# In the FFNs of a two-layer decoder trunk, block products are issued in pairs: wide halves together, narrow halves together, evacuations after

## The chip, the cores and the metric

The kernel runs on one core of one Trainium2 chip. The metric is the device time of one execution in microseconds (us), the median of several. PE is TensorE (matmuls), DVE is VectorE, ACT is ScalarE, POOL is GpSimd, SP is SyncE, which here issues DMAs. PSUM is the memory that PE writes its sums to, in banks of 512 columns of float32.

## The reference, cut to what matters

512 tokens of 1024 channels go through two layers. Each has a mixer and then a gated FFN of hidden width 2816:

```
def gated_conv_ffn(x, w_gate, w_up, conv_w, conv_b, w_down):
    g = jnp.einsum('bsd,df->bsf', x, w_gate)
    g = causal_dwconv3(g, conv_w) + conv_b
    up = jnp.einsum('bsd,df->bsf', x, w_up)
    return jnp.einsum('bsf,fd->bsd', jax.nn.silu(g) * up, w_down)
```

All of it is float32. In layer 0 the input is normalised by a factor of each token that the kernel multiplies in after the matmuls (`self.r`); in layer 1 the same, with one of the factors put into the last add.

## The kernel before, in words

**Precision.** A float32 factor is split in a high part and a low part, each of type float32r. A product of two such factors is made of three matmuls: high x high, high x low, low x high. The low part is either made by DVE as source minus high part (L153, L732, about 1.2 us for 128x1024), or by ACT's negated copy and a DMA that POOL issues, which adds the source (L142 to L144).

**Units of the FFN.** The 22 blocks of 128 hidden channels are taken two at a time: a unit `f` is blocks f and f + 1, for the gate ("g") and for the up-projection ("u"). Unit 0 is multiplied directly. Units 2 to 20 are multiplied by a scheme of seven block products in place of eight (2x2 blocks: halves of the 1024 input channels, and the two hidden blocks, against halves of the 512 tokens). The products are numbered 1 to 7. The sums of weight blocks which they need (s12, s34) are made by DVE (L752 to L775), split by ACT and DVE or by ACT and DMA, and sums of the input are made once a layer.

**A product** (`multiply`, L558 to L583) has four steps over the input channels, and adds into a PSUM bank: products 1, 6, 7 and 4 into bank "a", 5 and 3 into "e", 2 into "b", for g and u each their own. From unit 4 on for g and unit 6 for u (and three products of u in unit 4) the product is *wide*: four matmuls of 512 columns, in which the high weights meet high and low input at once (L571), then four of 256 columns, low weights with high input, into the first half of the bank (L574). Before that all twelve are 256 wide (L581).

**Evacuation** (`after`, L804 and L816). Since later products go on adding into the same bank, what it holds after each is read out: ACT copies the first half (products 1, 6, 5 and 4) and DVE adds the second half; for 2, 7 and 3 DVE adds both halves onto an earlier result. `rows` is the padded buffer of the gate, `kept` that of the up-projection. The next product into that bank has to wait for these reads.

**Order.** The products of a unit are written down as g1, u1, g2, g5, g6, u5, u6, g7, u2, u7, g3, u3, g4, u4, each with its evacuation straight behind it (L819 to L831). A scheduler then lays out the instructions of all engines by its own estimate of when each is ready; only instructions marked so keep program order. Each engine runs its list in order. After each unit from the second on comes a half of a down-projection of four earlier blocks (`half_down`: 48 matmuls of 512 columns, 12 into each of four banks), whose weights come in two chunks, each with a high split on ACT and a low split on DVE (L152, L153). There are seven banks in a pool for all of these.

**Buffers of the split weights.** High and low parts have six buffers each (`whi`, `wlo`), used in turn: a split waits until the matmuls that read the buffer's former contents are done.

Of the kernel before, what the change touches and what calls it, by code (L numbers as in the profile page):

```python
# [31 lines left out]
def tile_trunk(ctx: ExitStack, tc: tile.TileContext, x, norm_mix, norm_ffn, final_norm,  # L32
# [3 lines left out]
    nc = tc.nc  # L36
# [9 lines left out]
    def mm_bank(name):  # L46
        return ps_mm.tile([P, 512], F32, tag="mm", name=name)
# [240 lines left out]
    def padded_tile():  # L288
        turn[0] += 1
        return padded[turn[0] % NPADDED]  # L290
# [258 lines left out]
    NP = NK // 2  # L549
# [6 lines left out]
    last_matmul = [None]  # L556

    def multiply(banks, name, product, left, right, both=None):  # L558

        at = BANK[product]
        first = at not in banks
        if first:
            banks[at] = mm_bank(f"{name}{at}")
        ps = banks[at][:, :HALF]
        if both is not None:
            for kp in range(NP):  # L570
                nc.tensor.matmul(banks[at], left(kp)[0], both(kp), start=first and kp == 0,  # L571
                                 stop=kp == NP - 1, skip_group_check=True)
            for kp in range(NP):
                last_matmul[0] = nc.tensor.matmul(ps, left(kp)[1], right(kp)[0], start=False,  # L574
                                                  stop=kp == NP - 1, skip_group_check=True)
            return banks[at]
        for kp in range(NP):
            (a_hi, a_lo), (b_hi, b_lo) = left(kp), right(kp)
            for l, r, end in ((a_hi, b_hi, False), (a_hi, b_lo, False),
                              (a_lo, b_hi, kp == NP - 1)):  # L580
                nc.tensor.matmul(ps, l, r, start=first, stop=end, skip_group_check=True)  # L581
                first = False
        return ps  # L583

    def ffn_weights(layer, f, order):
        cs = slice(f * P, (f + 2) * P)
# [5 lines left out]
    class Ffn:  # L592
# [192 lines left out]
        def products(self, f, stat):  # L785

            layer, ap, n = self.layer, self.ap, f"{self.layer}_{f}"
            banks = {"g": {}, "u": {}}
            kept = ap.tile([P, 3, HALF], F32, tag="kept", bufs=1, name=f"kept{n}")
            pads = [padded_tile() for _ in range(2)]  # L790
            lo, hi = slice(2, 2 + HALF), slice(2 + HALF, 2 + S)
            dst = {("g", 1): pads[0][:, lo], ("g", 6): pads[0][:, hi], ("g", 7): pads[1][:, hi],
                   ("g", 4): pads[1][:, lo]}
            dst.update({("u", product): kept[:, i, :] for i, product in enumerate((1, 6, 7))})
            onto = {2: 1, 7: 7, 3: 6}
            s = {}

            def in_both(key, product):
                return f >= FIRST_WIDE[key] or f == FIRST_WIDE["g"] and product in (2, 5, 3)

            def add(d, bank, halves):
                ins = None
                for half in halves:
                    ins = nc.vector.tensor_tensor(d, bank[:, half * HALF : (half + 1) * HALF], d,  # L804
                                                  ALU.add)
                return ins

            def after(key, product, bank):
                halves = range(1 + in_both(key, product))
                if product in onto:  # L810
                    ins = add(dst[key, onto[product]], bank, halves)
                    if product == 7:
                        self.added[key] = ins
                elif (key, product) != ("u", 4):
                    d = dst[key, 7 if product == 5 else product]
                    nc.scalar.copy(d, bank[:, :HALF])  # L816
                    add(d, bank, halves[1:])

            for key, product in (("g", 1), ("u", 1), ("g", 2), ("g", 5), ("g", 6), ("u", 5),  # L819
                                 ("u", 6), ("g", 7), ("u", 2), ("u", 7), ("g", 3), ("u", 3),  # L820
                                 ("g", 4), ("u", 4)):
                bank = self.multiply(banks[key], f"{key}{n}", product, stat[key, product],
                                     in_both(key, product))
                after(key, product, bank)
                if (key, product) in (("g", 4), ("g", 3)):
                    j = product == 4
                    row = pads[j][:, 2:]
                    nc.vector.tensor_tensor(row, row, self.r, ALU.mult)  # L828
                    s[j] = self.silu(self.conv(pads[j], f + j), f + j)
                    if j and layer == 0:  # L830
                        nc.vector.tensor_tensor(s[1], s[1], self.r, ALU.mult)  # L831
            if layer == 0:
                nc.vector.tensor_tensor(kept[:, :2, :], kept[:, :2, :],
                                        self.r.rearrange("p (a b) -> p a b", a=2), ALU.mult)
            s0 = s[0].rearrange("p (a b) -> p a b", a=2)
            nc.vector.tensor_tensor(s0, kept[:, :2, :], s0, ALU.mult)
            nc.vector.tensor_tensor(s[1][:, HALF:], kept[:, 2, :], s[1][:, HALF:], ALU.mult)
            last = bank[:, :HALF]
            if in_both("u", 4):
                last = kept[:, 0, :]  # L840
                nc.scalar.copy(last, bank[:, :HALF])
                add(last, bank, (1,))
            nc.vector.tensor_tensor(s[1][:, :HALF], last, s[1][:, :HALF], ALU.mult)
            return [(f + 1, s[1]), (f, s[0])]
# [53 lines left out]
    def mixer1(norm):  # L898
        w = w_in_odd[0]
        with tc.tile_pool(name="m1", bufs=1) as mp:  # L900
# [27 lines left out]
            banks = v_group(0, {(4, 0): lambda: norm.rstd_cols(inorder)})  # L928
# [33 lines left out]
            def tokens(product, i):  # L962

                def at(kp):
                    if product in SUM:
                        cs = slice(i * P, (i + 1) * P)
                        return tuple(x[:, kp % 2, SUM[product], cs] for x in sums[kp // 2])
                    k = kp if product == 1 else kp + NP
                    cs = slice((i + 2 * (product == 4)) * P, (i + 2 * (product == 4) + 1) * P)
                    return hg[k][0][:, cs], hg[k][1][:, cs]  # L970
                return at

            class InProducts:
# [31 lines left out]
                def run(self, out_, done, behind_first):  # L1005
                    banks = ({}, {})
                    e = {}
                    for i, product in ((0, 1), (1, 1), (0, 2), (1, 2), (0, 6), (1, 6), (0, 5),
                                       (0, 7), (1, 5), (1, 7), (0, 4), (0, 3), (1, 4), (1, 3)):
                        if (i, product) == (0, 2):  # L1010
                            behind_first()
                        hi, lo = self.stat[product]
                        ps = multiply(banks[i], f"{self.name}_{i}", product, tokens(product, i),
                                      lambda kp: (hi[:, kp, :], lo[:, kp, :]))
                        c = {1: (0, 0), 2: (0, 0), 6: (0, 1), 3: (0, 1), 7: (1, 1), 5: (1, 1),
                             4: (1, 0)}[product]
                        dst = out_(i + 2 * c[0])[:, c[1] * HALF : (c[1] + 1) * HALF]
                        if product in (1, 6):
                            nc.scalar.copy(dst, ps)
                        elif product == 5:  # L1020
                            e[i] = ps
                        elif product == 7:
                            nc.scalar.copy(dst, ps)
                            nc.vector.tensor_tensor(dst, e[i], dst, ALU.add)
                            gelu(dst, dst, i + 2)
                        elif product == 4:
                            gelu(dst, ps, i + 2)
                            done(i + 2)
                        else:
                            nc.vector.tensor_tensor(dst, ps, dst, ALU.add)  # L1030
                        if product == 3:
                            row = out_(i)
                            gelu(row, row, i)
                            done(i)

            def gelu(dst, src, t):
                nc.scalar.activation(dst, src, AF.Gelu, scale=norm.cols[:, t : t + 1])
# [26 lines left out]
            u, gt, mix = {}, {}, {}  # L1064
# [334 lines left out]
    n = mixer0()  # L1399
    n = ffn0(n)  # L1400
    n = mixer1(n)
# [31 lines left out]
```

## Time and profile before

| | |
|---|---|
| median of 3 runs | 975.62 us (975.47 to 975.7) |
| span of the profiled execution, first to last instruction | 973.0 us |
| what lies around the span, against the median | 2.6 us |
| granted TensorE clock, mean | 0.998 |
| layer 0's FFN, units 2 to 20 | about 168 to 460 us |
| layer 1's FFN, units 2 to 20 | about 651 to 945 us |

The profile is of one execution; its own time is the span, and the runs are 2.6 us longer. In a line of the timeline stand the start in us from the span's start, the length in us, engine, line, operation, what is written and read, shape and count of the merged instructions, and in brackets the idle time before and what ended it. The length of a matmul is modelled and overlaps the next one; starts are what can be relied on. Buffer and layer numbers are left out of names: `g_12a` is bank "a" of g in unit 12, `whi_s12g` the high part of g's sums s12. A line of windows has the stretch, then busy time and count of PE, PEld (weight loads), DVE, ACT and POOL, then clock and DMA.

### The profile page before, as it was taken

To read this page: it belongs to the slowest core of one execution; us is meant where nothing else is said; L and a number is where in the kernel's file an instruction comes from. 1 tells how busy PE (TensorE), PEld (TensorE's weight loads), DVE (VectorE), ACT (ScalarE), POOL (GpSimd) and SP (SyncE) were. 2 spreads that over 40 slices of the span, in tenths; PEclk is the share of its full clock that TensorE was granted. 3 is DMA by queue.
4 is the path that set the end of the run, shared out by engine and by line. 5 is a ranking of instruction groups with operands and counts; after the bars stand their busy time and mean duration, and the time that the engine had idled before them with its cause. 6 is when DMAs were issued, how large, how long until landed. Compare 5 with 4: busy or idle time off the path is not lost.

```text
span 973.0 us, 14003 instructions
## 1 busy us (share of the span) xinstructions
PE 963.6 (99%) x5120; PEld 828.8 (85%) x5120; DVE 817.0 (84%) x1393; ACT 598.7 (62%) x905; POOL 149.9 (15%) x173
## 2 busy tenths in 40 slices
PE   9999999999999999999999999999999999999996
PEld 7888888988888888888889988889888888888885
DVE  5887458999899898998986865589998989889897
ACT  5523347765676665765487734587765667656775
POOL 2142023110111010110310001221111011100123
PEclk9999999999999999999999999999999999999999
DMA  7442225776777677774324623167767777668775
GB/s 251 146 139 86 87 88 108 178 178 165 195 178 181 146 178 185 174 174 140 119 58 110 221 67 99 55 132 187 186 145 194 196 173 172 156 165 201 194 153 140
DMA packets 94417, 148.36 MB, mean 152 GB/s; under 512 B 5156, under 2 KB 60428, under 8 KB 94348
## 3 DMA queue, kind: packets, MB, share of 16 engines
q1 hardware_dynamic: 78316, 98.69, 32.2%
q0 software_dynamic: 14256, 46.93, 26.7%
q10 hardware_dynamic: 1776, 1.84, 0.6%
q8 instruction: 40, 0.66, 0.3%
q14 instruction: 29, 0.24, 0.1%
HBM read 98.42 MB, written 2.10 MB: 103 GB/s over the span
## 4 chain that ended last, share of the span: by engine, by line
PE 99%; DVE 1%; issue 0%; ACT 0%; POOLq 0%; DVEq 0%; POOL 0%
PE dn L158 3%; PE d L158 3%; PE dn L159 3%; PE dn L157 3%; PE d L159 3%; PE d L157 3%; PE gu L157 2%; PE gu L159 2%; PE oo L159 1%; PE oo L157 1%; PE gu L158 1%; PE oe L157 1%; PE oe L159 1%; PE oo L158 1%; PE oe L158 1%; PE u_2a L581 1%
## 5 line engine op out<-in xcount | busy, mean ns | idle before, releaser
L617 DVE SCALAR_TENSOR_TENSOR c<-rows,prm,c 128x512 f32<-128x512 f32 x88 | 65.6, 748 | 1.5 <-ACT c L615 1.4
L144 POOL DMA_DIRECT2D wlo_g<-raw_g x20 | 17.2, 860 | 321.3 <-DVE kept L804 187.4
L158 PE MATMUL dn<-wlo_dn,a_hi 128*128 128x512 f32 x144 | 56.3, 391 | 0.0
L158 PE MATMUL d<-a_lo,whi_d 128*128 128x512 f32 x144 | 56.3, 391 | 0.0
L159 PE MATMUL dn<-whi_dn,a_lo 128*128 128x512 f32 x144 | 56.2, 391 | 0.0
L159 PE MATMUL d<-a_hi,wlo_d 128*128 128x512 f32 x144 | 56.2, 390 | 0.0
L157 PE MATMUL d<-a_hi,whi_d 128*128 128x512 f32 x144 | 56.2, 390 | 0.0
L157 PE MATMUL dn<-whi_dn,a_hi 128*128 128x512 f32 x144 | 56.2, 390 | 0.0
L731 ACT ACTIVATE whi_a<-raw_g 128x512 fp32r<-128x512 f32 x20 | 12.6, 631 | 61.0 <-PE g_10e L571 8.7
L213 POOL TENSOR_TENSOR ssq_f<-ssq_f,sq_f 128x512 f32<-128x512 f32 x14 | 19.8, 1411 | 134.4 <-ACT sq_f L212 99.5
L202 ACT ACTIVATE hg<-h,prm 128x512 fp32r<-128x512 f32 x24 | 17.3, 722 | 34.9 <-DVE h L315 34.9
L142 ACT ACTIVATE wlo_g<-raw_g 128x1024 fp32r<-128x1024 f32 x20 | 21.2, 1062 | 27.5 <-PE g_2e L581 8.8
L615 ACT ACTIVATE c<-rows,prm 128x512 f32<-128x512 f32 x44 | 31.3, 715 | 6.6 <-DVE rows L828 6.6
L1187 DVE SCALAR_TENSOR_TENSOR y<-dn,small,y 128x512 f32<-128x512 f32 x40 | 28.0, 749 | 8.6 <-PE dn L159 8.6
L625 ACT ACTIVATE s<-c,prm 128x512 f32<-128x512 f32 x44 | 31.4, 715 | 6.2 <-DVE c L617 6.1
L203 DVE SCALAR_TENSOR_TENSOR hg<-h,prm,hg 128x512 fp32r<-128x512 f32 x24 | 23.6, 986 | 11.1 <-ACT hg L202 11.1
L266 ACT ACTIVATE a_hi<-s 128x512 fp32r<-128x512 f32 x40 | 24.9, 627 | 11.4 <-PE d L159 7.7
L159 PEld LDWEIGHTS dn<-whi_dn,a_lo 128*128 128x128 f32 x144 | 27.1, 188 | 5.7
L159 PEld LDWEIGHTS d<-a_hi,wlo_d 128*128 128x128 f32 x144 | 27.1, 188 | 5.6
L153 DVE TENSOR_TENSOR wlo_dn<-raw_dn,whi_dn 128x1024 fp32r<-128x1024 f32 x18 | 22.0, 1224 | 11.7 <-ACT whi_dn L152 11.7
L157 PEld LDWEIGHTS dn<-whi_dn,a_hi 128*128 128x128 f32 x144 | 27.1, 188 | 5.3
L157 PEld LDWEIGHTS d<-a_hi,whi_d 128*128 128x128 f32 x144 | 27.1, 188 | 5.3
(1132 smaller groups left out, 3319.9 us busy)
## 6 DMA issues: line engine op xcount, KB each, us to landing
raw_g<-in_w_ffn_gate_dram SPq DMA_DIRECT2D x40, 512.0 KB, 3.8
raw_u<-in_w_ffn_up_dram SPq DMA_DIRECT2D x40, 512.0 KB, 4.0
raw_dn<-in_w_ffn_down_dram SPq DMA_DIRECT2D x22, 512.0 KB, 6.3
wlo_u<-raw_u POOLq DMA_DIRECT2D x21, 512.0 KB, 6.1
wlo_g<-raw_g POOLq DMA_DIRECT2D x20, 512.0 KB, 4.6
raw_d<-in_w_ffn_down_dram SPq DMA_DIRECT2D x18, 512.0 KB, 4.2
wlo_s12g<-s12g POOLq DMA_DIRECT2D x18, 512.0 KB, 6.3
wlo_s34g<-s34g POOLq DMA_DIRECT2D x18, 512.0 KB, 5.5
```

The source lines that it names most:

```text
L142: first = nc.scalar.activation(lo, raw, AF.Copy, scale=-1.0)
L153: behind(nc.vector.tensor_tensor(lo, raw, hi.bitcast(F32), ALU.subtract), after[0])
L157: nc.tensor.matmul(ps, lhs[0], rhs[0], start=start, stop=False)
L158: nc.tensor.matmul(ps, lhs[0], rhs[1], start=False, stop=False)
L159: nc.tensor.matmul(ps, lhs[1], rhs[0], start=False, stop=stop)
L203: nc.vector.scalar_tensor_tensor(hg[k][1], h[k], g, hg[k][0].bitcast(F32), op0=ALU.mult, op1=ALU.subtract)
L213: nc.gpsimd.tensor_tensor(self.ssq, self.ssq, sq, ALU.add)
L266: nc.scalar.activation(hi, src, AF.Copy, scale=scale)
L615: nc.scalar.activation(c, t[:, 0:S], AF.Copy, scale=prm("cf", ft))
L617: self.last_conv = nc.vector.scalar_tensor_tensor(c, t[:, i : S + i], prm("cf", i * NF + ft), c, op0=ALU.mult, op1=ALU.add)
L625: self.last_silu = nc.scalar.activation(s, c, AF.Silu, bias=self.prm("bf", ft))
L1187: return nc.vector.scalar_tensor_tensor(dst, ps, ffn.cols[:, t : t + 1], dst, op0=ALU.mult, op1=ALU.add)
```

## The change

`multiply` no longer issues the narrow matmuls of a wide product itself. It returns the bank and a function `low` that does. The caller takes the products two by two: first `multiply` of both, then `low` of both, then the evacuations of both. For a product that isn't wide, `multiply` does all twelve matmuls and `low` does nothing. The other caller (the mixer of layer 1) has only such products. What is computed stays the same, matmul by matmul.

```
@@ multiply
         if both is not None:
+
+            def low():
+                for kp in range(NP):
+                    last_matmul[0] = nc.tensor.matmul(ps, left(kp)[1], right(kp)[0], start=False,
+                                                      stop=kp == NP - 1, skip_group_check=True)
+
             for kp in range(NP):
                 nc.tensor.matmul(banks[at], left(kp)[0], both(kp), start=first and kp == 0,
                                  stop=kp == NP - 1, skip_group_check=True)
-            for kp in range(NP):
-                last_matmul[0] = nc.tensor.matmul(ps, left(kp)[1], right(kp)[0], start=False,
-                                                  stop=kp == NP - 1, skip_group_check=True)
-            return banks[at]
+            return banks[at], low
...
-        return ps
+        return ps, lambda: None
@@ products
-            for key, product in (("g", 1), ("u", 1), ("g", 2), ("g", 5), ("g", 6), ("u", 5),
-                                 ("u", 6), ("g", 7), ("u", 2), ("u", 7), ("g", 3), ("u", 3),
-                                 ("g", 4), ("u", 4)):
-                bank = self.multiply(banks[key], f"{key}{n}", product, stat[key, product],
-                                     in_both(key, product))
+            def finished(key, product, bank):
                 after(key, product, bank)
                 if (key, product) in (("g", 4), ("g", 3)):
...
+            for pair in ((("g", 1), ("u", 1)), (("g", 2), ("g", 5)), (("g", 6), ("u", 5)),
+                         (("u", 6), ("g", 7)), (("u", 2), ("u", 7)), (("g", 3), ("u", 3)),
+                         (("g", 4), ("u", 4))):
+                begun = [(key, product, *self.multiply(
+                    banks[key], f"{key}{n}", product, stat[key, product],
+                    in_both(key, product))) for key, product in pair]
+                for key, product, bank, low in begun:
+                    low()
+                for key, product, bank, low in begun:
+                    finished(key, product, bank)
```

In the kernel after, the wide matmuls are line L577, the narrow ones L573, ACT's copy L819 and DVE's adds L807.

More of the change, by code (lines that the diff above doesn't have):

```diff
@@ L1012, in run @@
                         hi, lo = self.stat[product]
-                        ps = multiply(banks[i], f"{self.name}_{i}", product, tokens(product, i),
-                                      lambda kp: (hi[:, kp, :], lo[:, kp, :]))
+                        ps, _ = multiply(banks[i], f"{self.name}_{i}", product,
+                                         tokens(product, i),
+                                         lambda kp: (hi[:, kp, :], lo[:, kp, :]))
                         c = {1: (0, 0), 2: (0, 0), 6: (0, 1), 3: (0, 1), 7: (1, 1), 5: (1, 1),
```

## The prediction

> **What bounds the kernel now.** I read the head of the page first, then the chain of waits, then the list of who waited for whom on PE.
>
> ```profile
> span 973.0 us, 14003 instructions
> ...
> PE 963.6 (99%) x5120; PEld 828.8 (85%) x5120; DVE 817.0 (84%) x1393; ACT 598.7 (62%) x905; POOL 149.9 (15%) x173
> ...
> PE 99%; DVE 1%; issue 0%; ACT 0%; POOLq 0%; DVEq 0%; POOL 0%
> ```
>
> ```profile
> PE clock L61 <- DVE idle L56: 1.3, 1, 1.3
> PE z L441 <- ACT hg L409: 0.3, 1, 0.3
> ```
>
> The chain that ends last is PE for 99% of the span, and in the whole run PE is seen to wait twice, both times at the start. So PE's stream of matmuls is the time. A change can gain only by making matmuls follow each other faster, and it loses whatever it makes PE wait. The median of the runs is 975.62 us, 2.6 us over this execution's span; I add my sum to the median.
>
> A busy PE is not PE at its peak, so I go by the starts in PE's timeline. Unit 2 of layer 0 is all 256 columns wide, a down-projection is all 512 wide, and unit 4 begins mixed:
>
> ```profile
> 168.02 0.40 PE L581 MATMUL g_2a<-hg,whi_a 128*128 128x256 f32 x2
> ...
> 188.17 0.40 PE L157 MATMUL d<-a_hi,whi_d 128*128 128x512 f32 x1
> ...
> 190.01 0.39 PE L159 MATMUL d<-a_hi,wlo_d 128*128 128x512 f32 x1
> ...
> 193.64 1.07 PE L571 MATMUL g_4a<-hg,whi_a 128*128 128x512 f32 x4
> 194.54 0.64 PE L574 MATMUL g_4a<-hg,wlo_a 128*128 128x256 f32 x4
> ...
> 196.46 1.09 PE L571 MATMUL g_4b<-hg,whi_g 128*128 128x512 f32 x4
> ```
>
> From 168.02 to 188.17 stand the 168 matmuls of unit 2: 0.120 us each. From 190.01 to 193.64 stand 16 of 512 columns: 0.227 us each. These are the two plain rates. Now a wide unit, number 12 of layer 1:
>
> ```profile
> 796.78 0.64 PE L574 MATMUL g_12b<-hg,wlo_g 128*128 128x256 f32 x4
> 797.26 1.09 PE L571 MATMUL g_12e<-t,whi_s12g 128*128 128x512 f32 x4
> ...
> 798.66 1.09 PE L571 MATMUL g_12a<-t,whi_s12g 128*128 128x512 f32 x4
> 799.59 0.64 PE L574 MATMUL g_12a<-t,wlo_s12g 128*128 128x256 f32 x4
> 800.06 1.09 PE L571 MATMUL u_12e<-t,whi_s12u 128*128 128x512 f32 x4
> 800.99 0.63 PE L574 MATMUL u_12e<-t,wlo_s12u 128*128 128x256 f32 x4
> 801.46 1.09 PE L571 MATMUL u_12a<-t,whi_s12u 128*128 128x512 f32 x4
> 802.39 0.64 PE L574 MATMUL u_12a<-t,wlo_s12u 128*128 128x256 f32 x4
> 802.87 1.09 PE L571 MATMUL g_12a<-t,whi_s34g 128*128 128x512 f32 x4
> ...
> 805.68 0.63 PE L571 MATMUL u_12a<-t,whi_s34u 128*128 128x512 f32 x2
> ```
>
> Five products (four matmuls of each width) go from 798.66 to 805.68, 7.02 us. At the plain rates they would take 5 x (4 x 0.227 + 4 x 0.120) = 6.94. So a round trip from 512 columns to 256 and back costs about 0.017 us. It hardly depends on how long the stretches are: 188.17 to 196.46 is one trip with 28 wide and 16 narrow matmuls, 8.29 us, against 28 x 0.227 + 16 x 0.120 = 8.28 (8.27 with the unrounded rate), so 0.01 to 0.02. There is nothing else to gain in this stream.
>
> **What the change removes: round trips.** No matmul is added or taken away. In the two built programs I counted how often a run of 512-column matmuls is followed by one of 256: 247 times before, 157 after. It is not seven fewer in each unit, because the scheduler breaks up the middle pairs; in nine units it puts three of product u6's narrow matmuls ahead of g7's wide ones and the fourth behind them. 90 trips at 0.017 us are 1.5 us. The longer runs may cost a little more each (0.019 against 0.017, the top of what the one long trip allows): 157 x 0.002 = 0.3 back. I take a gain of **1.2 us**, bounds 0 and 1.5. The Trainium skill, "TensorE: Matmul & The Clock Gate", section "Back-to-back issue gap", gives the warm spacing as N/2.4 + 2.5 ns, set by the columns alone; its 216 and 109 ns lie under the 227 and 120 of this trace. By that rule a trip costs nothing and this gain would be 0.
>
> **What the change adds: two shorter deadlines.** Products that add into the same bank must wait until the one before is read out. Only two such distances get short. Product g7 goes into the bank of g6, u7 into that of u6. Before, two whole products lie between: from 800.06 (g6's stream ends) to 802.87, 2.81 us. After, between the end of g6 and the start of g7 lie u5's narrow half (0.47, from 800.99 to 801.46), u6's wide half (0.93, 801.46 to 802.39) and three narrow matmuls (0.36): **1.76 us**. For u7 it is the same: g7's narrow half, u2's wide half and three narrow ones of u2. The others stay long: g6 after g1 has two products (2.8 us) and a half, g4 after g7 four products, u4 after u7 two products and more, and the down-projections take banks that were read earlier.
>
> What must be done in that time is seen in the rows of DVE (first fence) and ACT (second):
>
> ```profile
> 797.46 0.89 DVE L804 TENSOR_TENSOR rows<-g_12b,rows 128x256 f32<-128x256 f32 x2 [0.43 <-PE g_12b L574]
> ...
> 800.93 1.23 DVE L153 TENSOR_TENSOR wlo_dn<-raw_dn,whi_dn 128x1024 fp32r<-128x1024 f32 x1 [1.12 <-ACT whi_dn L152]
> 802.07 0.42 DVE L804 TENSOR_TENSOR rows<-g_12a,rows 128x256 f32<-128x256 f32 x1
> ...
> 803.73 1.23 DVE L153 TENSOR_TENSOR wlo_dn<-raw_dn,whi_dn 128x1024 fp32r<-128x1024 f32 x1 [0.91 <-ACT whi_dn L152]
> 804.88 0.42 DVE L804 TENSOR_TENSOR kept<-u_12a,kept 128x256 f32<-128x256 f32 x1
> ```
>
> ```profile
> 799.83 1.06 ACT L152 ACTIVATE whi_dn<-raw_dn 128x1024 fp32r<-128x1024 f32 x1 [0.55 <-PE g_12a L571]
> 800.80 0.36 ACT L816 COPY rows<-g_12a 128x256 f32<-128x256 f32 x1
> ...
> 802.64 1.06 ACT L152 ACTIVATE whi_dn<-raw_dn 128x1024 fp32r<-128x1024 f32 x1 [0.61 <-PE u_12a L571]
> 803.61 0.35 ACT L816 COPY kept<-u_12a 128x256 f32<-128x256 f32 x1
> ```
>
> ACT copies one half of the bank, DVE adds the other. Ahead of g6's add stands DVE's 1.23 us split of the down-projection's weights (wlo_dn, L153), before and after; it writes the buffer in which g6's low weights lie, so it can't begin until g6's narrow half has ended. Before, this kept g6's add at 802.07 to 802.49, 2.43 us after g6's end, and just within the 2.81. In the order built from the changed kernel the split stands ahead of g6's add in nine wide units (16 and 20 of layer 0, 8 to 20 of layer 1), and the second split ahead of u6's add in those nine and in units 8 and 12 of layer 0.
>
> The chain after, from the end of g6's stream: DVE begins 0.20 later (g2's stream ends at 797.26 and the add that idled for it starts at 797.46). The split takes 1.23, the add starts 0.09 before its end (802.07 against 802.16) and takes 0.42: done at 1.76. The high split on ACT is not in the way: it waits for g6's wide half, which after the change ends 0.93 us earlier relative to the narrow one, and the copy of 0.36 fits beside DVE's split. What PE loses when such an add is late is seen in unit 10 of layer 0, DVE's row first:
>
> ```profile
> 289.63 0.42 DVE L804 TENSOR_TENSOR rows<-g_10a,rows 128x256 f32<-128x256 f32 x1
> ```
>
> ```profile
> 289.76 0.39 PE L571 MATMUL u_10b<-hg,whi_u 128*128 128x512 f32 x1
> 290.10 1.20 PE L571 MATMUL g_10a<-t,whi_s34g 128*128 128x512 f32 x4
> 291.13 0.40 PE L574 MATMUL g_10a<-t,wlo_s34g 128*128 128x256 f32 x2
> ```
>
> The add ends at 290.05, PE goes on at 290.10: 0.05 later. Then the four wide matmuls take 1.03 us where those at 798.66 take 0.93: 0.10 more, the restart. So the first matmul counts as started at 1.76 + 0.05 + 0.10 = 1.91, against a free slot at 1.76: **0.15 to 0.16 us lost at each wait**. The Trainium skill, same page, section "Step-by-step: what each phase is for", says that PE pulls weight loads ahead of matmuls in flight; by that the restart would be hidden and each wait would cost some 0.05. The 1.03 us in unit 10 speaks against it for a weight load that itself has to wait.
>
> Behind the waiting matmul on PE stands all the rest of the unit, so the loss goes through to the end; behind the split on DVE stand g6's add and u5's, and only PE waits for them. ACT and DVE take their next work from PE's results, so they shift along and gain no further delay.
>
> Number of waits: two in nine units, one in units 8 and 12 of layer 0, and one in units 14 and 18 of layer 0, where g6's add stands directly behind the split of the sums s34u, which itself comes later (behind the copy of u1); that one I can only estimate, between 0 and 0.6 us, and give it the same price. 22 x 0.16 = **3.5 us**. Bounds: nothing, if the chain is 0.16 us shorter than read; 22 x 0.3 = 6.6, if DVE comes to the split 0.15 us late. Unit 10 has no such wait after the change (all of u2's wide half lies between): its 0.11 + 0.10 = 0.2 us go.
>
> **Costed at nothing.** Moved evacuations: ACT and DVE do the same instructions in another order, hidden behind PE. POOL's and SP's orders are the same, so no transfer passes another. Later evacuation of g3 and g4 is covered by the down-projection (52 wide matmuls, about 11.8 us) before the next unit; without that cover it would cost up to 0.93 us a unit.
>
> **Sum.** + 3.5 - 1.2 - 0.2 = + 2.1 us: span 975.1, median **977.7 us**, 0.21% slower. My own range for this case is 976.5 to 979.2. About 0.2% (1.95 us) is what a measurement of this kernel can tell from no change.
>
> **Rivals.** (1) *The deadlines are met.* The chain of five readings is 0.16 us longer than the slot; if DVE's split begins or ends that much earlier, all 22 waits vanish together, and PE keeps the saved trips: - 1.2 - 0.2, 974.2 us, not slower. For it: the scheduler placed three narrow matmuls exactly so that its own reckoning has no wait. Against it: the row of unit 10. Chance 0.18, with 0.05 for still more saved per trip. (2) *Trips cost nothing*: then what I read as a trip is a cost of each matmul in mixed stretches, and regrouping saves 0: 978.9 us. Against it: the long trip above costs no more than the short. Chance 0.12. The formula of the Trainium skill that is named above ("TensorE: Matmul & The Clock Gate", "Back-to-back issue gap") would lead to this rival's time. (3) *DVE falls behind.* In these stretches it has little room, in layer 0 less than in layer 1 (third busy figure, of 50 us):
>
> ```profile
> 300.00:350.00 50.00, 50.00 (x258) 42.72 (x257) 46.67 (x83) 34.24 (x50) 6.03 (x7) 1.00 0.77 179
> ...
> 750.00:800.00 50.00, 50.00 (x260) 42.72 (x259) 45.12 (x81) 33.77 (x50) 6.88 (x8) 1.00 0.77 181
> ```
>
> If evacuating in pairs puts one more operation of 1.22 us ahead of g6's add in the eight wide units of layer 0, that is 8 x 1.2 = 9.8 us more: 987 us. Chance 0.15. (4) The pairs are not formed: excluded, the built order has 157 trips.
>
> **How the numbers follow.** Forecast 0.50, (1) 0.23, (2) 0.12, (3) 0.15. The range 974.0 to 983.0 leaves out most of (3) and the 0.05 of (1). Slower by over 0.2% (above 977.57): 0.28 of the forecast's 0.50, nearly all of (2), all of (3), together 0.55 to 0.57. Faster by over 0.2% (below 973.67): 0.07. The rest, 0.37, lies within.
>
> **What would show it.** Right: starts of g7 and u7 some 0.15 us after their slot in the nine units, about 0.05 us after DVE's L807 add on rows or kept, then a long first matmul; L153 directly before that add; pairs of 8 wide and 8 narrow matmuls in 2.79 us instead of 2.81. Wrong: PE without gaps at g7 (rival 1), pairs still at 2.81 (rival 2), gaps of a microsecond in layer 0 alone (rival 3), or PE waiting in a place that I have costed at nothing, such as the first product of a unit.

## The result, and the profile after

The changed kernel takes **980.69 us** (median of 4 runs, 979.92 to 981.17), beside 975.55 us for the kernel before (4 runs, 975.03 to 975.7): 1.0054 times as long, interval 1.0041 to 1.0067. That is 5.1 us more in the medians; the spans of the two profiled executions differ by 5.6 us. The run behind the profile after took 980.52 us for a span of 978.6, 1.9 us more; by that the execution behind the profile before, with its span of 973.0, was itself some 0.6 us quicker than its median (an estimate), and that is how 5.6 and 5.1 go together. The forecast was 2.1 us more: the side and the kind were right, and the forecast size was less than half of the measured one. The time lies above the 976.5 to 979.2 that I gave for the case itself. It lies inside the wide range, which was made to leave room for a part of rival 3.

The head of the page, and the chain that ended last:

```profile
span 978.6 us, 14010 instructions
...
PE 968.0 (99%) x5120; PEld 829.2 (85%) x5120; DVE 813.4 (83%) x1393; ACT 597.9 (61%) x905; POOL 150.6 (15%) x173
...
PE 94%; DVE 4%; DMA 1%; issue 0%; ACT 0%; POOLq 0%; DVEq 0%; POOL 0%
```

The same number of matmuls; PE's share of the chain went from 99% to 94%, DVE's from 1% to 4%. PE's list of waits (engine, line, what it waited for, us in total, times, longest) is the next thing to look at:

```profile
PE clock L61 <- DVE idle L56: 1.3, 1, 1.3
PE g_14a L577 <- DVE rows L807: 0.9, 1, 0.9
PE dn_a L1292 <- DVE y L1198: 0.2, 1, 0.2
```

Two of these are new, and together they are 1.1 of 5.6 us. The other 4.5 are not in the list: the waits behind them are too short for it, and they show only in the starts of the matmuls. I took the time of each unit from the start of its first matmul to the start of what follows its last one. Against before: +0.33 to +0.37 us in each of units 8 to 20 of layer 1 (2.46 us for seven), +0.34 to +0.36 in units 8, 12, 16 and 20 of layer 0, **+1.07 in unit 14** of layer 0, +0.13 in its unit 18, -0.13 in its unit 10; units 4 and 6 are 0 to 0.08 shorter. That makes 4.8 us. What follows unit 20 of layer 1 takes 38.86 us in place of 38.15: +0.7.

The same unit as in the forecast, number 12 of layer 1, PE's timeline after:

```profile
799.03 1.09 PE L577 MATMUL g_12b<-hg,whi_g 128*128 128x512 f32 x4
...
801.82 1.09 PE L577 MATMUL g_12a<-t,whi_s12g 128*128 128x512 f32 x4
802.75 1.07 PE L577 MATMUL u_12e<-t,whi_s12u 128*128 128x512 f32 x4
803.66 0.64 PE L573 MATMUL g_12a<-t,wlo_s12g 128*128 128x256 f32 x4
804.13 0.64 PE L573 MATMUL u_12e<-t,wlo_s12u 128*128 128x256 f32 x4
804.61 1.09 PE L577 MATMUL u_12a<-t,whi_s12u 128*128 128x512 f32 x4
805.54 0.52 PE L573 MATMUL u_12a<-t,wlo_s12u 128*128 128x256 f32 x3
806.00 1.19 PE L577 MATMUL g_12a<-t,whi_s34g 128*128 128x512 f32 x4
807.04 0.28 PE L573 MATMUL u_12a<-t,wlo_s12u 128*128 128x256 f32 x1
```

and beside it DVE's, then one row of ACT:

```profile
804.39 1.23 DVE L153 TENSOR_TENSOR wlo_dn<-raw_dn,whi_dn 128x1024 fp32r<-128x1024 f32 x1 [1.15 <-ACT whi_dn L152]
805.53 0.42 DVE L807 TENSOR_TENSOR rows<-g_12a,rows 128x256 f32<-128x256 f32 x1
```

```profile
803.00 1.06 ACT L152 ACTIVATE whi_dn<-raw_dn 128x1024 fp32r<-128x1024 f32 x1 [0.55 <-PE g_12a L577]
```

A pair (8 wide, 8 narrow) takes 2.79 us, from 799.03 to 801.82, where two products took 2.81. The narrow matmuls of g6 (bank `g_12a`, from 803.66) have all been issued by 804.13. The split of the down-projection's weights begins at 804.39, 0.26 us behind that, and so it does in all nine units. (Its bracket names ACT's high split, but that had ended at 804.06, 0.33 us earlier.) g6's add ends at 805.95; g7 starts at 806.00, which is 0.46 behind the first of three narrow matmuls that take 0.36 at the plain rate; and its four matmuls take 1.04 in place of 0.93. So g7 is 0.10 to 0.11 late and pays 0.10 for the restart: **0.21 us a wait**, with the split directly ahead of the add, as forecast. u7 repeats it. Two waits are 0.42, five saved trips give 0.07 back: the +0.35 of the unit.

What the restart is, the weight loads show (PEld, the same stretch):

```profile
801.70 0.78 PEld L577 LDWEIGHTS g_12a<-t,whi_s12g 128*128 128x128 f32 x4
...
806.00 0.76 PEld L577 LDWEIGHTS g_12a<-t,whi_s34g 128*128 128x128 f32 x4 [0.15 <-DVE rows L807]
```

The first load for g6 begins at 801.70, 0.12 us ahead of its matmul at 801.82, while the matmul before it is still under way. The load for g7 waits for the add like the matmul itself and begins with it, at 806.00, so it is no longer hidden.

### The profile page after: what moved, and what is told of

Its sections match the earlier page's. It is cut to its first block, busy times and chain, and to the rows that moved or that the text cites. A ratio compares the mean times of both kernels' runs of the same rounds, so it can differ in the third digit from the quotient of the medians.

```text
span 978.6 us, 14010 instructions
## 1 busy us (share of the span) xinstructions
PE 968.0 (99%) x5120; PEld 829.2 (85%) x5120; DVE 813.4 (83%) x1393; ACT 597.9 (61%) x905; POOL 150.6 (15%) x173
## 4 chain that ended last, share of the span: by engine, by line
PE 94%; DVE 4%; DMA 1%; issue 0%; ACT 0%; POOLq 0%; DVEq 0%; POOL 0%
PE dn L157 3%; PE dn L158 3%; PE dn L159 3%; PE d L158 3%; PE d L157 3%; PE d L159 3%; PE gu L157 2%; PE gu L159 1%; PE oo L159 1%; PE oo L157 1%; PE gu L158 1%; PE oe L159 1%; PE oe L158 1%; PE oo L158 1%; PE oe L157 1%; PE u_2a L584 1%
## 5 line engine op out<-in xcount | busy, mean ns | idle before, releaser
L158 PEld LDWEIGHTS dn<-wlo_dn,a_hi 128*128 128x128 f32 x144 | 27.1, 188 | 5.2
L158 PEld LDWEIGHTS d<-a_lo,whi_d 128*128 128x128 f32 x144 | 27.1, 188 | 5.2
```

The source lines that it names most:

```text
L158: nc.tensor.matmul(ps, lhs[0], rhs[1], start=False, stop=False)
```

## The experiments

Eleven more kernels ran, each timed beside the kernel before (medians of 974.98 to 975.21 us in these). Of each change only the lines that matter are shown, with pairs written as product names. A theory and a rival stand ahead of each run.

**1. Only the four outer pairs** (178 trips), and **2. only the three middle pairs** (227 trips). The two halves of the change:

```
 outer:   pairs g1 u1, g2 g5, g3 u3, g4 u4; g6, u5, u6, g7, u2, u7 singly
 middle:  pairs g6 u5, u6 g7, u2 u7; all others singly
```

> Only the pairs g1-u1, g2-g5, g3-u3 and g4-u4 are formed; g6, u5, u6, g7, u2, u7 go singly as before. 178 round trips against 247 before and 157 in the change. Theory (the loss is PE waiting for the evacuation of g6 and u6, everything else about pairs is a small gain): no waits at g7 and u7, 69 trips at 0.012 to 0.017 us saved, 974.4 to 974.9 us, 0.7 to 1.2 under before. Rival (reading out two products at once disturbs ACT and DVE whatever the pair): four of seven pairs, so four sevenths of the loss, about 978.5 us.

Measured: 974.23 us (973.76 to 975.0), ratio 0.9992 (0.9983 to 1.0001): 0.2 below the theory's range, and not clear of before. The wide units are 0.03 to 0.06 us shorter than before, but for units 8 (0.00) and 10 (+0.26, its old wait at g7, now longer) of layer 0.

> The opposite part: only g6-u5, u6-g7 and u2-u7 are pairs. 227 round trips. Theory: all the waits of the change are there and few trips are saved; between 979.5 and 981.5 us, with g7 and u7 each 0.2 us late in the units from 8 on. Rival: three sevenths of the loss, about 977.8 us.

Measured: 980.87 us (979.37 to 982.63), ratio 1.0057 (1.0044 to 1.0069). The whole loss is in the middle pairs, and what the outer pairs bring is small, as the theory has it. The sum inside differs: units 8 to 20 of layer 1 are 0.40 to 0.43 longer, there is no loss in unit 14 and none at the end, but 1.5 us in unit 18 of layer 0 (number 7 comes back to it) and 0.6 in unit 10.

**3. Other middle pairs**, so that each bank's two accumulations keep two products between them (132 trips):

```
-  (g6 u5), (u6 g7), (u2 u7)
+  (g6 u6), (u5 u2), (g7 u7)
```

> All seven pairs, in an order in which no product follows closely on one of the same bank: g1-u1, g2-g5, g6-u6, u5-u2, g7-u7, g3-u3, g4-u4. 132 round trips. Theory: g7 and u7 have a whole pair and more between them and the product before in their bank, so no waits; 115 trips saved at 0.012 to 0.017 us: 973.6 to 974.2 us, below before. Rival (bunched evacuation): as the change, 980 to 981 us.

Measured: **1009.61 us** (1006.42 to 1009.87), ratio 1.0345 (1.0331 to 1.0359). Both numbers missed, by about 30 us and more. Layer 1 does what the theory says: no waits, wide units 0.09 us shorter than before. Layer 0's units 10 to 20 are 4.4 to 6.5 us longer each. PE's waits in it:

```profile
PE g_10e L573 <- DMA wlo_s12g<-s12g: 2.4, 1, 2.4
PE u_20b L573 <- DMA wlo_u<-raw_u: 2.3, 1, 2.3
PE g_14e L573 <- DMA wlo_s12g<-s12g: 2.2, 1, 2.2
...
PE g_14a L577 <- DVE rows L807: 2.1, 1, 2.1
```

The rows point to the scheduler's order: in it DVE makes s34g, and in units 10, 14 and 18 the last sum of s12g too, behind the whole of the down-projection's adds, so the low weights that a transfer makes from them come late. In unit 14 the last sum of s12g begins 2.0 us after the unit's first matmul; before, it began 16.0 us ahead of it. No run put that order back, so this cause is read and not tested. A new order of products changes DVE's list beyond the products that were regrouped, and in layer 0 that costs far more than the deadlines at issue.

**4. The change, with each of the two splits put behind the add** that it stood ahead of:

```
+  split_after = {}          # product 6 of g, u -> its add
-  hi, lo = weights(...)
+  hi, lo = parts(*fetch(...), after=(split_after.pop(i // 2, None), None))
...
+  if product == 6: split_after["gu".index(key)] = ins
```

> The change, with DVE's low split of the down-projection's two weight chunks put behind the add of g6 and that of u6. 137 round trips. Theory (the 1.2 us split ahead of the add in DVE's order makes the evacuation too late): the 20 waits of 0.21 us behind that split go, the wait of 1.1 us in unit 14 of layer 0 stays: 975.5 to 976.7 us. Rival (the way from PE over ACT and DVE back to PE is itself too long for the slot): the waits stay, 980 to 981 us.

Measured: 976.81 us (975.58 to 977.75), ratio 1.0014 (1.0005 to 1.0023): a shade above the theory's range, 3 us from the rival's. In layer 1 units 8 to 20 are now 0.09 to 0.10 us shorter than before, so the split ahead of the add is the whole of that loss. Layer 0 keeps some, as PE's list shows:

```profile
PE g_14a L580 <- DVE rows L810: 0.9, 1, 0.9
PE u_8a L580 <- DVE kept L810: 0.7, 1, 0.7
PE dn_a L1297 <- DVE y L1203: 0.2, 1, 0.2
```

Unit 14 (+1.06), the end (+0.71) and new losses in units 8 (+0.95), 18 (+0.43) and 12 (+0.25) are of another kind.

**5. The change, with u2 and u7 singly.** Are the two waits of a unit independent?

```
-  (u2 u7)
+  (u2), (u7)
```

> The change with u2 and u7 each by itself, the six other pairs kept. Theory (each late add costs 0.21 us by itself, and u7's is met once all of u2 stands between: from u6's end g7's narrow half 0.47 and u2 whole 1.40 are 1.87 us, against 1.76 for the split and the add and 0.05 for the handing over): one wait is left in the wide units of layer 1, at g7, and they go from +0.36 to +0.15 us against before; units 8 and 12 of layer 0 lose u7's wait too; 978.2 us (977.7 to 978.9). Rival (the two waits are tied: u7 is late because g7 was, or g7's grows when u7's goes): units stay at +0.30 us or more, 980 us or above.

Measured: 977.26 us (976.61 to 977.75), ratio 1.002 (1.0011 to 1.003). The wide units with the split ahead of both adds are +0.20 to +0.23, between the theory's +0.15 and the rival's +0.30; the median is below the theory's range, because the 0.7 at the end and the 1.1 of unit 14 went too. Its unit 12 of layer 1, PE and then DVE:

```profile
806.28 0.63 PE L573 MATMUL u_12b<-hg,wlo_u 128*128 128x256 f32 x4
806.77 1.20 PE L577 MATMUL u_12a<-t,whi_s34u 128*128 128x512 f32 x4
807.80 0.63 PE L573 MATMUL u_12a<-t,wlo_s34u 128*128 128x256 f32 x4
```

```profile
805.15 1.23 DVE L153 TENSOR_TENSOR wlo_dn<-raw_dn,whi_dn 128x1024 fp32r<-128x1024 f32 x1 [1.12 <-ACT whi_dn L152]
806.29 0.42 DVE L807 TENSOR_TENSOR kept<-u_12a,kept 128x256 f32<-128x256 f32 x1
```

The add ends at 806.71 and u7 starts at 806.77, 0.01 us behind its slot (806.28 and four times 0.12): the deadline is met, as worked out. Yet its four matmuls take 1.03 us, not 0.93. **The restart is paid even where PE stood still for only 0.01 us.** That is why the expected +0.15 became +0.21. g7's own wait is as long as in the change, so the two waits are independent.

**6. The change, with g1 and u1 singly.** I had put unit 14's loss down to u1's copy and add, which in a pair stand ahead of the weights s12u:

```
-  (g1 u1)
+  (g1), (u1)
```

> The change with g1 and u1 each by itself, the other five pairs kept. Theory for unit 14 of layer 0 (u1's evacuation, moved to the end of the pair, stands on ScalarE and VectorE ahead of the weights s12u and pushes the chain s12u, s34u, g6's add behind g7's time): unit 14 goes from +1.07 us against before to between +0.2 and +0.45 us (its two common waits stay), all other units longer by 0.01 to 0.02 us for one pair fewer, so 980.2 us (979.8 to 980.5). Rival (the chain is late because of g6 and u5 as a pair, u1's place doesn't count): unit 14 stays at +1.0 us or more and the time is 980.8 to 981.1 us.

Measured: 980.66 us (979.42 to 981.1), ratio 1.0052 (1.0039 to 1.0064). Unit 14 lost nothing (-0.05), but unit 8 lost 1.6 us at another place, the start of u4. DVE's rows there, then PE's:

```profile
265.95 0.69 DVE L755 TENSOR_TENSOR s12g<-raw_g,raw_g 128x512 f32<-128x512 f32 x1 [3.56 <-DMA raw_g<-in_w_ffn_gate_dram]
...
268.16 0.41 DVE L807 TENSOR_TENSOR kept<-u_8a,kept 128x256 f32<-128x256 f32 x1
```

```profile
268.63 0.73 PE L577 MATMUL u_8a<-t,whi_u 128*128 128x512 f32 x2 [1.23 <-DVE kept L807]
```

u7's add stands behind a sum for the next unit, and that sum idles 3.56 us for its weights' transfer. And the theory of u1's place falls: in this kernel, as in number 5, u1's copy and add still stand ahead of the weights s12u in unit 14, and nothing is lost. What differs is when DVE comes to them: it begins the last of these sums (L757) 3.7 us after the unit's first matmul in the change, 2.0 us after it in both of these, with the same list of operations from that sum to g6's add. PE's losses of 2.1 us in units 8 and 10 may have let DVE catch up here, so another test was needed.

**7. The change with less work for DVE in layer 0.**

```
-  if layer == 0:
-      nc.vector.tensor_tensor(kept[:, :2, :], kept[:, :2, :],
-                              self.r.rearrange("p (a b) -> p a b", a=2), ALU.mult)
```

> The change, without the multiplication of kept by the tokens' factor in layer 0 (0.69 us of VectorE in each of its units; that part of the computation is left out). Theory for unit 14 of layer 0 (VectorE comes into the unit late: in the change it reaches the sums s12u 3.71 us after g1's first matmul, where the runs with first products apart and with u7 apart, which have u1's copy and add in the same place, reach them at 2.0 and lose nothing): with 0.69 us less in each unit it reaches them at 3.0 us or sooner, and unit 14 goes from +1.07 to between -0.05 and +0.45 us; layer 1's units and the end stay as they are; 979.3 to 980.2 us. Rival (u1's copy and add ahead of the weights s12u decide): unit 14 stays at +0.9 us or more, 980.3 to 981.0 us.

Measured: 979.97 us (979.63 to 980.38), ratio 1.0051 (1.0038 to 1.0065). Unit 14 goes from +1.07 to +0.36, within the theory's range: two common waits and no more. Here are DVE's last sum and low split of s12u and what leads to g6's add, then PE's first product and g7, in this run:

```profile
338.72 0.69 DVE L757 TENSOR_TENSOR s12u<-s12u,raw_u 128x512 f32<-128x512 f32 x1
...
343.89 1.22 DVE L735 TENSOR_TENSOR wlo_s12u<-s12u,whi_s12u 128x1024 fp32r<-128x1024 f32 x1
...
350.01 1.23 DVE L153 TENSOR_TENSOR wlo_d<-raw_d,whi_d 128x1024 fp32r<-128x1024 f32 x1 [0.50 <-ACT whi_d L152]
351.15 0.42 DVE L807 TENSOR_TENSOR rows<-g_14a,rows 128x256 f32<-128x256 f32 x1
```

```profile
341.88 1.07 PE L577 MATMUL g_14a<-hg,whi_a 128*128 128x512 f32 x4
...
351.63 1.19 PE L577 MATMUL g_14a<-t,whi_s34g 128*128 128x512 f32 x4
```

and in the change:

```profile
345.44 0.68 DVE L757 TENSOR_TENSOR s12u<-s12u,raw_u 128x512 f32<-128x512 f32 x1
...
347.25 1.23 DVE L735 TENSOR_TENSOR wlo_s12u<-s12u,whi_s12u 128x1024 fp32r<-128x1024 f32 x1 [0.46 <-ACT whi_s12u L734]
...
351.14 1.22 DVE L735 TENSOR_TENSOR wlo_s34u<-s12u,whi_s34u 128x1024 fp32r<-128x1024 f32 x1 [0.46 <-ACT whi_s34u L734]
352.28 0.42 DVE L807 TENSOR_TENSOR rows<-g_14a,rows 128x256 f32<-128x256 f32 x1
```

```profile
352.75 1.19 PE L577 MATMUL g_14a<-t,whi_s34g 128*128 128x512 f32 x4 [0.87 <-DVE rows L807]
```

The split of s12u begins 2.0 us into the unit (343.89 against 341.88) instead of 5.5 us (347.25 against a unit start of 341.74). In the change, ScalarE's and DVE's splits of s12u and then of s34u follow one another with DVE's sums between them, and g6's add stands behind the last.

But this run changed more than the lag. The scheduler moved the last sum of s12u to 3.2 us ahead of the unit's first matmul (338.72 against 341.88; the theory had asked for 3.0 us after it or sooner), and put the split of the down-projection's weights ahead of g6's add, in units 10, 14 and 18 alike. So it can't tell a smaller lag from a better order. Six runs can: in these DVE's list from that sum to g6's add is the same in unit 14, and in unit 18 too, and only the time differs at which DVE comes to it.

| unit of layer 0, run | the last sum of s12u begins, us after the unit's first matmul | the unit against before, us |
|---|---|---|
| 14, numbers 5, 6 and 2 | 2.01, 2.02, 2.21 | -0.05, -0.05, -0.01 |
| 14, number 8 | 3.36 | +0.74 |
| 14, number 4 | 3.67 | +1.06 |
| 14, the change | 3.71 | +1.07 |
| 18, numbers 8 and 6 | 2.61, 2.62 | -0.02, -0.01 |
| 18, the change | 2.79 | +0.13 |
| 18, number 4 | 3.04 | +0.43 |
| 18, number 2 | 4.12 | +1.51 |

With the list the same, the loss follows the lag, nearly us for us once DVE is more than about 2.6 us late. So unit 14 is DVE's lag in layer 0, the third rival of the prediction, in one unit. The gain of number 7 in the total is only 0.7 us, since with its order units 10 and 18 take the two common waits each (+0.14 and +0.36, in unit 10 less the wait that it had before).

**8. The change, with unit 20 of layer 1 issued singly.**

```
+  if layer == 1 and f == 20:
+      pairs = tuple((p,) for pair in pairs for p in pair)
```

> The change, but unit 20 of layer 1, the last before the final products, issues its products singly. Theory (the 0.7 us that the end loses come from VectorE work of this one unit that ends later and is passed on to the final products): the stretch behind unit 20 goes from 38.86 back to about 38.15 us and the unit from +0.33 to 0: 979.6 us (979.4 to 979.9). Rival (the end is longer because VectorE's order there or the backlog from earlier units differs): only the unit's 0.33 go, 980.3 us, and the stretch stays above 38.7 us.

Measured: 978.82 us (978.65 to 979.28), ratio 1.0036 (1.0024 to 1.0049). The end is back at 38.15 us and the unit at 0.00, both as the theory says; the median is 0.6 below its range. Layer 0 is written as in the change, and yet unit 14 lost 0.74 in place of 1.07, and units 8 and 12 together 0.3 less. What the end looks like in the change, PE then DVE:

```profile
962.75 0.39 PE L1292 MATMUL dn_a<-whi_dnp,hg 128*128 128x512 f32 x1
963.37 0.50 PE L1292 MATMUL dn_a<-whi_dnp,hg 128*128 128x512 f32 x1 [0.23 <-DVE y L1198]
963.71 0.40 PE L1292 MATMUL dn_a<-wlo_dnp,hg 128*128 128x512 f32 x1
```

```profile
962.57 0.74 DVE L1198 SCALAR_TENSOR_TENSOR y<-dn_a,small,y 128x512 f32<-128x512 f32 x1
```

From one start to the next are 0.62 us where 0.23 is plain, and 0.34 after it: 0.5 us of the 0.7, a bank that DVE has not yet read out. The last unit's late evacuations stay with DVE through the final products: counted from the end of the unit on PE, the add of u4 begins at 6.19 us in the change and at 5.26 in number 8, and the read-out shown here at 22.84 against 22.01. Which pair does it is open: the end is 38.12 to 38.14 us in numbers 1, 2 and 5, where only some of the pairs are formed, and 38.85 to 38.88 in numbers 3, 4 and 11, where the last unit itself loses nothing.

**9. More trips, the order of products left alone.** Before, with each product as two wide, two narrow, two wide, two narrow:

```
-  4 wide, 4 narrow
+  for k0 in (0, 2):  2 wide (k0, k0 + 1), 2 narrow (k0, k0 + 1)
```

> The kernel before, with each wide product issued as two matmuls of 512 columns, two of 256, two of 512, two of 256: 492 trips between the widths in place of 247, the evacuations where they were. Theory (a trip costs time of its own, 0.013 us by the units of the pairs that kept their deadlines, 0.017 by the gaps that the prediction took): 245 trips more are 3.2 to 4.2 us, so 978.7 to 979.8 us and a wide unit of layer 1 longer by about 0.15 us (11 or 12 trips more). Rival (only columns count): 975.5 us, no unit longer by over 0.03.

Measured: **973.52 us** (972.73 to 974.1), ratio 0.9981 (0.9972 to 0.999): faster than before, with twice the trips. Both numbers missed, on the same side. A wide unit of layer 1 is 0.06 to 0.10 us shorter than before.

I had taken it that no deadline gets shorter here. One does. ACT's high split of the down-projection's weights waits for the last wide matmul of g6, which in unit 12 of layer 1 now starts 0.93 us after g6's first in place of 0.70. DVE's split and g6's add follow: the add ends 0.11 us ahead of g7 in place of 0.38, and g7's second matmul comes 0.27 us behind its first in place of 0.23. Most wide units pay these 0.04 us.

**10. One wide, one narrow, by turns.**

```
-  4 wide, 4 narrow
+  for kp in range(NP):  1 wide (kp), 1 narrow (kp)
```

> The kernel before, with the two widths taking turns within a wide product: 512, 256, 512, 256 and so on, some 980 trips between the widths. Theory by places (new, from the starts in layer 1 of before and of the run with two and two: the first matmul of 512 columns behind one of 256 takes 0.234 us, the first of 256 behind one of 512 takes 0.115, whatever comes further on): a turn is 0.349 us, as long as half a round of two and two, so wide units of layer 1 of 19.54 us and 973.2 to 973.9 us in all. Rival (every trip has a price above the plain rates, 0.004 us by the run with two and two): 0.351 us a turn, units of 19.66 us, 975.4 to 975.9 us. The old price of 0.013 us a trip would give 0.360 us and 982 us.

Measured: 977.89 us (977.85 to 979.83), ratio 1.0032 (1.0019 to 1.0044): outside the ranges of both theories, and well short of the 982 of the old price. Its unit 12 of layer 1, and below it that of the run with two and two:

```profile
795.25 0.40 PE L571 MATMUL g_12a<-hg,whi_a 128*128 128x512 f32 x1
795.48 0.28 PE L573 MATMUL g_12a<-hg,wlo_a 128*128 128x256 f32 x1
...
798.78 0.40 PE L571 MATMUL g_12b<-hg,whi_g 128*128 128x512 f32 x1
...
809.12 0.39 PE L571 MATMUL g_12e<-hg,whi_s34g 128*128 128x512 f32 x1
...
814.67 0.39 PE L157 MATMUL dn<-whi_dn,a_hi 128*128 128x512 f32 x1
```

```profile
792.28 0.63 PE L572 MATMUL g_12a<-hg,whi_a 128*128 128x512 f32 x2
792.75 0.39 PE L575 MATMUL g_12a<-hg,wlo_a 128*128 128x256 f32 x2
...
795.07 0.63 PE L572 MATMUL g_12b<-hg,whi_g 128*128 128x512 f32 x2
```

Ten turns take 3.53 us (795.25 to 798.78), 0.353 each. The last sixteen turns of the same unit take 5.55 (809.12 to 814.67), 0.347 each, which is what the plain rates give: there a trip costs nothing. Four rounds of two and two take 2.79 (792.28 to 795.07), 0.349 for one matmul of each width. So above the plain rates a trip costs 0.006 us or nothing at one and one, about 0.004 at two and two, 0.016 at four and four (7.02 us for five products, in the forecast) and 0.014 at eight and eight (2.79 us a pair, above, against 8 x 0.227 + 8 x 0.120 = 2.776). A trip has no price of its own: it depends on the length of the runs, and at one and one not on that alone. What in PE makes it so stays open.

Nor is the total of number 10 a matter of trips alone. The last wide matmul of g6 starts 1.06 us after its first, g6's add ends 0.06 us ahead of g7, and the whole restart of 0.10 us is paid. Its units are 3.4 us longer than before, and such late starts, with a wait of 0.5 us for weights in unit 6 of layer 0, come to 1.8 us in them, against 0.3 before.

**11. The pairs that suit each layer:** those of number 1 in layer 0, those of number 3 in layer 1.

```
+  pairs = outer if layer == 0 else by_bank
```

> Layer 0 with the pairs that keep every deadline there (g1 and u1, g2 and g5, g3 and u3, g4 and u4; the six others singly), layer 1 with g1 u1, g2 g5, g6 u6, u5 u2, g7 u7, g3 u3, g4 u4, where each bank's two accumulations stay two products apart. Theory (short deadlines are the loss, trips the gain): layer 0 as in the run with outer pairs alone, layer 1's wide units 0.09 us shorter than before in place of 0.05, so 973.8 us (973.4 to 974.2), below both kernels. Rival (pairs bring no gain that lasts to the end of the kernel, or the end grows by VectorE's backlog as in the change): 974.5 to 975.6 us.

Measured: 974.43 us (973.83 to 975.4), ratio 0.9992 (0.9983 to 1.0001). The wide units do what the theory says (-0.03 to -0.06 in layer 0 but for +0.05 in unit 10, -0.06 to -0.10 in layer 1). The end is 38.88 us: the 0.7 of the change are there again, as the rival had it, and the median lies between the two ranges. Number 9 remains the only version that is below both kernels by more than the noise: 1.7 us below the kernel before, measured beside it.

## Why the prediction was right, and where it was too small

- **PE's stream is the time, and what PE waits for goes through to the end:** right. The units' losses add up along the kernel to the difference of the spans.
- **Trips, -1.2 us:** right in size. Units without a wait are 0.05 us shorter for four trips fewer and 0.09 for seven, 0.013 a trip, so 90 trips are 1.2 us. The argument under it, one price per trip whatever the run's length, held for the runs of four and eight that it was read from and fails for shorter ones (numbers 9 and 10). Rival 2 fails: with seven trips fewer, units without a wait are shorter. The Trainium skill's formula ("TensorE: Matmul & The Clock Gate", "Back-to-back issue gap"), which that section calls the gap of a single isolated matmul, gives 0.325 us for one matmul of each width in any order; these traces have 0.347 to 0.353, by the order.
- **Two short deadlines, 22 waits:** right in place and in cause (numbers 2 and 4). The size of a wait was too small: 0.21 us, not 0.155. The term at fault is "DVE begins 0.20 later", which I took from an add; the split began 0.26 behind the end of g6's stream. The restart of 0.10 was right. The Trainium skill, same page, "Step-by-step: what each phase is for", has weight loads pulled ahead of matmuls in flight. The trace agrees where nothing waits (801.70 against 801.82) and not where a matmul waits for an add: its load begins with it (806.00), and number 5 paid the 0.10 even at 0.01 us of standing still. 21 waits at 0.05 more are about 1.1 us.
- **"That one I can only estimate, between 0 and 0.6 us":** unit 18 lost about what an ordinary wait costs (+0.13); unit 14 took 1.14 us (1.07, and 0.07 of trips), above the upper bound. The step looked at the order within the unit and not at when DVE comes to it, which decides (the table in number 7). It is rival 3, which I had priced for eight units and which came in one: about 1.0 us of the miss.
- **"u4 after u7 two products and more"** (stays long): wrong in units 8 and 12 of layer 0. u7's add is there one of several behind a sum that waits for a transfer, and u4 was late as well; in number 6 this alone is 1.2 us. In the change it is worth about 0.2 us each, 0.4 together.
- **Moved evacuations, costed at nothing:** wrong for the last unit. The cover that I named, PE's other work, was there for PE but not for DVE, which carries the delay into the final products: 0.7 us (number 8).
- **Unit 10's 0.2 us go:** only about 0.1 went. I had it that no wait is left there; g6's add still ends 0.06 us ahead of g7, and the restart is paid once more.

Forecast 2.1, and 1.1 + 1.0 + 0.4 + 0.7 + 0.1: 5.4 us, against 5.6 in the spans. The sum had 2.2 us of the loss at nothing or under too low a bound. That the time still lies in the wide range, which was left wide for rival 3, is in part luck.

## What to carry to other kernels

Before you regroup work that shares buffers, write down for each one the time between its last writer and its next writer, before and after, and hold it against the full chain that empties it, with what its engine's list puts ahead; a chain 0.06 us longer than read was a fifth of the price here. Then ask when that engine comes to the stage at all: in a kernel with one engine at 99% and another at 83%, the losses that were not foreseen were those of the second engine's lag, and a scheduler moves that lag with every edit. And look for a form of the edit that has the gain without the new deadlines: two and two within a product came close, and what it left of one deadline was 0.11 us in place of 0.38.

## What the runs showed of the hardware that was not expected

- What matmuls of two widths take depends on their order: 0.351 us for one of each at four and four, 0.349 at two and two and at eight and eight, and at one and one 0.353 or 0.347 in different parts of the same unit.
- A matmul that waits for another engine's add starts 0.05 to 0.06 us after that add's end, and its weight load starts no earlier, so the next matmul comes 0.10 us later than usual, even if PE would otherwise have been free only 0.01 us earlier.
- The cost fades as the add ends sooner. At g7 the second wide matmul comes 0.33 to 0.34 us behind the first when the add ended 0.05 to 0.06 us ahead of it. It comes at 0.29 with 0.10 us (unit 4 of layer 1 in the change) and at 0.26 with 0.13 (unit 8 of layer 0 before). With 0.18 it comes at 0.23, as usual (unit 18 of layer 0 before). So the cost ends somewhere between 0.13 and 0.18 us, and a deadline met by less than that still costs.
